# Gathering and scattering the experts' tokens with 128 rows in place of 96, the slots laid on partitions 0 to 31, 64 to 95 and 32 to 63

## The chip, the cores and the metric

The kernel runs on one core of one Trainium2 chip. The metric is the device time of one execution in microseconds (us); less is better. Three timed executions of the kernel before gave 757.03, 757.23 and 759.32 us; the median is 757.23 us.

## The reference, cut to what matters

One decoder layer for 512 prompt tokens and 32 sample tokens, T = 544 rows of D = 1024 numbers. After the attention and convolution branches and a first layer norm, each token goes through a routed mixture of 16 gated experts: a router picks one group of four experts, then two experts in it, so each token belongs to two experts and an expert has 2 * 544 / 16 = 68 tokens on average.

```python
def hier_moe(x, w_group, w_router, w1, w3, w2):
    t = x.reshape(N * S, D)
    gp = softmax(t @ w_group);  p_g, g_idx = top_k(gp, 1)
    ep = softmax((t @ w_router) of that group);  top_w, top_i = top_k(ep, 2)
    gate = one-hot sum of p_g * top_w / sum(top_w)           # (T, 16), two entries a row
    y = 0
    for e in range(16):                                      # D_EXPERT = 512
        y = y + gate[:, e:e + 1] * ((silu(t @ w1[e]) * (t @ w3[e])) @ w2[e])
x = layer_norm(ALPHA * x + hier_moe(x, ...), ln2_g, ln2_b)
```

All numbers are 32-bit floats. The weights of one expert are three matrices of 2 MB, 6 MB together (6.29 million bytes).

## The kernel before

Everything up to the first layer norm ends at about 450 us of the profiled span and is not touched, except for one small constant. The normed rows are written to a table in DRAM, `x1d`; a second table, `acc`, collects the experts' output.

**Routing.** For each token and expert the kernel has `pos`: 0 if the token does not go to the expert, otherwise its number in the expert's list, 1, 2, 3 and so on. An expert takes at most CAP = 96 tokens (a second path, not run here, treats any rest). `onehots(e)` compares `pos` with the constant `slot`, which holds 1 to 96 along the free axis, and so makes a 0/1 matrix of tokens by slots (tile `soh`). `place(e)` multiplies it with the token numbers on TensorE (L1110), and a vector operation (L1104) turns the result into row indices `gix`, one on each partition: partition p holds the token of slot p + 1. A slot without a token gets the index 1024, which is out of range; the indirect DMA has a bounds check, and such a row moves nothing. `gate_of(e, ...)` reduces the gate of each slot (L1097) and copies parts of it to other partitions with small ScalarE operations (L1099, L1101), for the use in `down`. For experts 0 and 1 `place_early` makes the indices alone, as soon as `pos` is there, and `gates_early` the gates later.

**One expert.** `gather(e)` (L1117, queue of GpSimd) reads the rows of `x1d` named by `gix` into `xg`, one row of 4 KB to a partition, 96 partitions. `x_t(e)` transposes them in 32 by 32 blocks on VectorE (L1209; on TensorE for expert 0, L1215). `up(e, ...)` multiplies with w1 and w3 on TensorE, 192 matmuls (L1229), in three rounds of 32 slots, g = 0, 1, 2; `glu` and `h_t` (L1242, L1243, L1248) make the hidden rows; `down(e, h)` multiplies with w2, 96 matmuls (L1260). Its result lies in PSUM in four partition groups of 32; six ScalarE operations (L1272, L1273 and four of L1275) scale it by the gate and bring it into `y`, 96 partitions of 4 KB. Then an indirect DMA (L1277, GpSimd) adds the rows of `y` to the rows of `acc` named by `gix`. Experts 14 and 15 make no scatter: their outputs stay in SBUF and are added by matmuls at the end (L1286, L1378, L1379).

**Order.** The program for expert e is up(e, first half), h_t(e - 1), x_t(e + 1), up(e, second half), place(e + 4) and gather(e + 4), down(e - 1), glu(e). TensorE therefore works in blocks of 192 + 96 matmuls, and the gather of an expert is issued some four experts ahead.

**Weights.** Each expert's weights come in six pieces of 1 MB: four for `up` (tile `we`, two DMAs of 512 KB each) and two for `down` (tile `wd`), all issued on SyncE's queue at L798. The pieces go round 20 buffers. From piece 21 on, a piece is issued only when the piece five before it has landed:

```python
behind = first if ring["n"] in GATED else loads[-1 - AHEAD] if ring["n"] > THR0 else None   # AHEAD = 5
```

**End.** The rows of `x1d` and `acc` are loaded into `z` (L1363, L1370, L1372; the ones from `acc` wait for the last scatter), added to the outputs of experts 14 and 15 on VectorE and ScalarE (L1426, L1430), normed and stored.

Of the kernel before, what the change touches and what calls it, by code (L numbers as in the profile page):

```python
# [18 lines left out]
F32 = mybir.dt.float32  # L19
F32R = mybir.dt.float32r  # L20
BF = mybir.dt.bfloat16
F16 = mybir.dt.float16
I32 = mybir.dt.int32
AF = mybir.ActivationFunctionType
ALU = mybir.AluOpType
AX = mybir.AxisListType.X
PSUM = bass.MemoryType.PSUM

D = 1024
# [4 lines left out]
NT = 5  # L34
# [3 lines left out]
NE = 16  # L38
# [6 lines left out]
CAP = 96  # L45
BIG = 1.0e30
FAR = 1024.0
# [31 lines left out]
YB = 2  # L79
NXG = 3  # L80
# [7 lines left out]
def layer_kernel(ctx: ExitStack, tc: tile.TileContext, i_, o_):  # L88
    nc = tc.nc
    mm = nc.tensor.matmul  # L90
# [33 lines left out]
    x1d = tc.dram_tile([T, D], F32, name="x1d")  # L124
    acc = tc.dram_tile([T, D], F32, name="acc")
    cdr = tc.dram_tile([NH, NPR], F32, name="cdr")

    const = ctx.enter_context(tc.tile_pool(name="const", bufs=1))
# [198 lines left out]
    with tc.issue_after(ln_done.ins):  # L327
# [13 lines left out]
    identb = const.tile([128, 128], BF, name="identb")  # L341
# [5 lines left out]
                            base=0, channel_multiplier=-1)  # L347
# [7 lines left out]
                            base=0, channel_multiplier=1)  # L355
    later = pa.tile([128, 128], F32, name="later")
    nc.gpsimd.affine_select(later, ones[:, :128], pattern=[[-1, 128]], compare_op=ALU.is_gt, fill=0.0,
                            base=0, channel_multiplier=1)
    before = const.tile([128, 128], BF, name="before")
    nc.gpsimd.affine_select(before, ones[:, :128], pattern=[[1, 128]], compare_op=ALU.is_gt, fill=0.0,  # L360
                            base=0, channel_multiplier=-1)
    rsel = pa.tile([NH, 4, NH, 4], F32, name="rsel")
    nc.gpsimd.affine_select(rsel, ones[:NH, :128].rearrange("p (a b c) -> p a b c", a=4, b=NH),
                            pattern=[[0, 4], [1, NH], [0, 4]], compare_op=ALU.is_equal, fill=0.0,
                            base=0, channel_multiplier=-1)
# [1 line left out]
    nc.gpsimd.iota(prow, pattern=[[0, 1]], base=0, channel_multiplier=1)  # L367
    pcol = const.tile([128, 1], F32, name="pcol")
    nc.vector.tensor_copy(pcol, prow)
    slot = const.tile([128, CAP], BF, name="slot")  # L370
    nc.gpsimd.iota(slot, pattern=[[1, CAP]], base=1, channel_multiplier=0,
                   allow_small_or_imprecise_dtypes=True)
    rn = pa.tile([128, 2], F32, name="rn")
    rni = pa.tile([128, 2], I32, name="rni")
    nc.vector.tensor_single_scalar(rni[:, 0:1], prow, 5, op=ALU.arith_shift_right)
# [4 lines left out]
                   allow_small_or_imprecise_dtypes=True)  # L380
    nc.gpsimd.iota(coln[:, 1], pattern=[[0, 8], [1, 4]], base=0, channel_multiplier=0,
                   allow_small_or_imprecise_dtypes=True)
    smask = pa.tile([128, 2, 32], BF, name="smask")
    for g in range(2):
        a = p1.tile([128, 32], F32, name="sma", tag="tra", bufs=2)
        b = p1.tile([128, 32], F32, name="smb", tag="trb", bufs=2)
        nc.vector.tensor_scalar(a, coln[:, 0].rearrange("p a b -> p (a b)"), -4.0 * g, rn[:, 0:1],
                                op0=ALU.add, op1=ALU.is_equal)
# [482 lines left out]
    xgs = []  # L871
# [21 lines left out]
    def small(name, shape, dt=F32):  # L893
        return p2.tile([128] + shape, dt, name=name)

    def bc(ap, k):
        return ap.unsqueeze(len(ap.shape)).to_broadcast(list(ap.shape) + [k])
# [189 lines left out]
    onehot = {}  # L1087

    def onehots(e):
        oh = p2.tile([128, NT, CAP], BF, name="soh", tag="soh", bufs=2)  # L1090
        nc.vector.tensor_tensor(oh, slot.unsqueeze(1).to_broadcast([128, NT, CAP]), bc(pos[:, :, e], CAP),
                                op=ALU.is_equal)
        onehot[e] = oh
        return oh

    def gate_of(e, parts):
        nc.vector.tensor_reduce(gat[:CAP, e:e + 1], parts, axis=AX, op=ALU.add)  # L1097
        if e < E0:
            nc.scalar.activation(gat2[64:, e, 0:1], gat[:64, e:e + 1], AF.Copy)  # L1099
            for q in range(4):  # L1100
                nc.scalar.activation(gat2[32 * q:32 * q + 32, e, 1:2], gat[64:96, e:e + 1], AF.Copy)  # L1101

    def to_index(e, me):
        return nc.vector.tensor_scalar(gix[:CAP, e:e + 1], me, FAR, None, op0=ALU.add)  # L1104

    def place(e):
        pmt = ps_s("pmt")
        oh = onehots(e)
        for x in range(NT):
            mm(pmt[:CAP, :5], oh[:, x], mv[:, x, e], start=x == 0, stop=x == NT - 1)  # L1110
        me = p2.tile([CAP, 1], F32, name="me", tag="me", bufs=2)
        nc.vector.tensor_reduce(me, pmt[:CAP, 0:2], axis=AX, op=ALU.add)
        to_index(e, me)
        gate_of(e, pmt[:CAP, 2:5])

    def gather(e):
        return nc.gpsimd.indirect_dma_start(out=xgs[e % NXG][:CAP], out_offset=None, in_=x1d,  # L1117
                                     in_offset=bass.IndirectOffsetOnAxis(ap=gix[:CAP, e:e + 1], axis=0),
                                     bounds_check=T - 1, oob_is_err=False)

    def place_early(e):
        oh = onehots(e)
        pm0 = ps_s("pm0")
        for x in range(NT):
            mm(pm0[:CAP, :1], oh[:, x], tokh[:, x:x + 1], start=x == 0, stop=x == NT - 1)
        return to_index(e, pm0[:CAP, :1]), gather(e)

    def gates_early(e):
        oh = onehot[e]
        pg0 = ps_s("pg0")  # L1130
        for x in range(NT):
            mm(pg0[:CAP, :3], oh[:, x], mv[:, x, e, 2:5], start=x == 0, stop=x == NT - 1)
        gate_of(e, pg0[:CAP, :3])

    gix0, first = place_early(0)
# [2 lines left out]

    gl = lgt[:, :, :NG]
    el = lgt[:, :, NG:]  # L1140
    oh1 = small("oh1", [NT, NE])
    oh2 = small("oh2", [NT, NE])
    nc.vector.scalar_tensor_tensor(oh1, rank[:, :, NG:], 0.0, asf, op0=ALU.is_equal, op1=ALU.mult)
    nc.vector.tensor_sub(oh2, asf, oh1)
    pick = p2.tile([128, NT, NE], F32, name="pick", tag="dv", bufs=2)
# [45 lines left out]
    nc.vector.tensor_reduce(flag[:1], pmT[:1, :128], axis=AX, op=ALU.max)  # L1191
    flagi = small("flagi", [1], I32)
    nc.vector.tensor_copy(flagi[:1], flag[:1])

# [59 lines left out]
    def down_round(r, py, h, raws, ks):  # L1256
        for k in ks:
            for q in range(4):
                g, c = (q % 2, 2 * (q // 2) + r) if r < 2 else (2, q)
                mm(py[32 * q:32 * q + 32, 256 * r:256 * r + 256], h[:, k, 32 * g:32 * g + 32],  # L1260
                   raws[k // 2][:, k % 2, 256 * c:256 * c + 256], start=k == 0 and r != 1, stop=k == 3,
                   skip_group_check=True)

    def down(e, h):
        y = p2.tile([CAP, D], F32, name="y", tag="y", bufs=YB)
        py = ps_mm("py").rearrange("p a b -> p (a b)")
        for j in range(2):
            raws = {j: raw_e(e, 4 + j)}
            for k in (2 * j, 2 * j + 1):
                for r in range(3):  # L1270
                    down_round(r, py, h, raws, (k,))
        nc.scalar.activation(y[:64, :512], py[:64, :512], AF.Copy, scale=gat[:64, e:e + 1])  # L1272
        nc.scalar.activation(y[:64, 512:], py[64:, :512], AF.Copy, scale=gat2[64:, e, 0:1])  # L1273
        for q in range(4):
            nc.scalar.activation(y[64:, 256 * q:256 * q + 256], py[32 * q:32 * q + 32, 512:768], AF.Copy,  # L1275
                                 scale=gat2[32 * q:32 * q + 32, e, 1:2])
        nc.gpsimd.indirect_dma_start(out=acc, out_offset=bass.IndirectOffsetOnAxis(ap=gix[:CAP, e:e + 1], axis=0),  # L1277
                                     in_=y, in_offset=None, bounds_check=T - 1, oob_is_err=False,
                                     compute_op=ALU.add)

# [8 lines left out]
    def onehots_t(e):  # L1289
        if not ohT:  # L1290
            ohT["all"] = pr_p.tile([CAP, KC, NT, 128], F32R, name="ohT", tag="pre", bufs=NPRE)
        ohp = psum.tile([CAP, NT, 128], BF, name="ohp", tag="o", bufs=1)
        for x in range(NT):
            nc.tensor.transpose(ohp[:, x], onehot[e][:, x], identb)
        ohT[e] = ohT["all"][:, e - E0]
        nc.vector.tensor_copy(ohT[e], ohp)

# [310 lines left out]
```

## Time and profile before

| what | value |
|---|---|
| median of three timed executions | 757.23 us (757.03 to 759.32) |
| the profiled execution's own time | 758.94 us |
| its span, first to last instruction | 757.2 us |
| mean granted TensorE clock | 0.987 of full speed |
| TensorE busy | 725.2 us, 96% of the span |
| DMA, mean over the span | 224 GB/s |
| chain that ended last | TensorE 68%, DMA 26%, VectorE 4% |

The page of the profile gives one execution. The busy share of TensorE is an average over stages that have different limits, and a busy TensorE is not one at its peak, since matmuls are pipelined. The time line of an engine shows runs of like instructions, with the idle time before a run in square brackets and what ended it. The DMA view of a stretch counts the packets that started in it, by queue: the loads of the weights run on q1 (issued by SyncE), the gathers and scatters on q0 (issued by GpSimd), and q8 fetches instructions. A packet's share is the time that it took; 100% stands for 16 DMA engines busy for the whole stretch, and shares add up to a little over 100% where packets of an engine overlap at their ends.

### The profile page before, as it was taken

The numbers are of one execution on the slowest core, as the hardware profiler recorded it, in microseconds if no ns is written. First come the engines' busy times: TensorE is split into PE (matmuls) and PEld (weight loads), VectorE is DVE, ScalarE is ACT, GpSimd is POOL, SyncE is SP. The second block draws the span as 40 slices with busy tenths as digits, with TensorE's granted clock in tenths as the row PEclk, the third lists the DMA queues.
The fourth block names the chain that finished last, engine by engine and source line by source line (L and its number), as shares of the span: only waits on it lengthen the run. The fifth ranks groups of instructions, "written<-read, shape, count | busy, mean of one in ns | idle before, by whom it ended". The sixth has DMA issues, their size and how long they took to land.

```text
span 757.2 us, 18645 instructions
## 1 busy us (share of the span) xinstructions
PE 725.2 (96%) x8102; PEld 563.8 (74%) x8102; DVE 354.3 (47%) x841; ACT 246.0 (32%) x502; POOL 114.7 (15%) x152
## 2 busy tenths in 40 slices
PE   7999999999999999999999998999999999898992
PEld 6899888898998999999975754656555565565551
DVE  3335667753435222333555684733454333441147
ACT  3443564533144222222423332322323322111234
POOL 5411000012441000000020521121111211100110
PEclk8999999999999999999999999999999999999997
DMA  9565302215552444434175589999999999999973
GB/s 226 188 219 173 108 29 82 70 50 194 168 168 85 144 131 147 168 112 167 57 277 182 203 327 341 339 370 337 358 371 334 363 360 338 343 375 376 386 177 121
DMA packets 65431, 169.65 MB, mean 224 GB/s; under 512 B 6144, under 2 KB 26672, under 8 KB 65344
## 3 DMA queue, kind: packets, MB, share of 16 engines
q1 hardware_dynamic: 55776, 141.08, 52.4%
q0 software_dynamic: 8992, 25.74, 12.8%
q8 instruction: 66, 1.08, 0.6%
q10 hardware_dynamic: 576, 1.57, 0.5%
q14 instruction: 21, 0.17, 0.1%
HBM read 157.40 MB, written 14.49 MB: 227 GB/s over the span
## 4 chain that ended last, share of the span: by engine, by line
PE 68%; DMA 26%; DVE 4%; issue 1%; SPq 0%; ACT 0%; DVEq 0%; ACTq 0%
DMA we<-in_w_dram 16%; PE pj L168 10%; PE pj L169 9%; PE pj L170 9%; DMA wd<-in_w_dram 8%; PE pab L1229 7%; PE py L170 2%; PE py L169 2%; PE py L168 2%; PE py L1260 2%; PE po L169 2%; PE po L170 2%; PE po L168 2%; PE py L1286 2%; PE S L566 1%; PE po L600 1%
## 5 line engine op out<-in xcount | busy, mean ns | idle before, releaser
L1229 PE MATMUL pab<-we,xgT 128*32 128x256 f32 x3072 | 172.3, 381 | 1.2 <-DMA we<-in_w_dram 1.0
L1229 PEld LDWEIGHTS pab<-we,xgT 128*32 128x32 f32 x3072 | 103.0, 111 | 65.3 <-issue 3.2
L1209 DVE STREAM_TRANSPOSE xgT<-xg 32x256 f32<-32x256 f32 x180 | 78.4, 435 | 117.1 <-PE pab L1229 106.4
L1260 PE MATMUL py<-wd,hT 128*32 128x256 f32 x1344 | 75.4, 380 | 4.5 <-DMA wd<-in_w_dram 2.9
L168 PE MATMUL pj<-xth,wgas 128*128 128x272 f32 x256 | 73.9, 289 | 0.0
L169 PE MATMUL pj<-xtl,wgas 128*128 128x272 f32 x256 | 73.9, 289 | 0.0
L170 PE MATMUL pj<-xth,wgas 128*128 128x272 f32 x256 | 73.6, 288 | 0.0
L1260 PEld LDWEIGHTS py<-wd,hT 128*32 128x32 f32 x1344 | 44.1, 110 | 30.7 <-ACT su L1242 3.8
L164 DVE TENSOR_TENSOR wgas<-wga,wgas 128x1024 fp32r<-128x1024 f32 x16 | 19.6, 1226 | 87.3 <-ACT wgas L163 87.3
L168 PEld LDWEIGHTS pj<-xth,wgas 128*128 128x128 f32 x256 | 48.3, 189 | 0.8 <-issue 0.8
L169 PEld LDWEIGHTS pj<-xtl,wgas 128*128 128x128 f32 x256 | 48.2, 188 | 0.0
L170 PEld LDWEIGHTS pj<-xth,wgas 128*128 128x128 f32 x256 | 48.2, 188 | 0.0
L1242 ACT ACTIVATE su<-pab 128x384 f32<-128x384 f32 x16 | 7.8, 490 | 104.8 <-PE pab L1229 104.8
L1277 POOL DMA_INDIRECT acc<-y,gix x14 | 20.1, 1439 | 129.0 <-ACT y L1275 129.0
L168 PE MATMUL pj<-xth,wqks 128*128 128x272 f32 x128 | 38.6, 302 | 0.0
L169 PE MATMUL pj<-xtl,wqks 128*128 128x272 f32 x128 | 36.9, 289 | 0.0
L170 PE MATMUL pj<-xth,wqks 128*128 128x272 f32 x128 | 36.9, 289 | 0.0
L163 ACT ACTIVATE wgas<-wga 128x1024 fp32r<-128x1024 f32 x16 | 16.9, 1055 | 47.4 <-DMA wga<-in_w_in_dram 46.5
L1117 POOL DMA_INDIRECT xg<-x1d,gix x16 | 15.7, 980 | 101.9 <-DVE gix L1104 76.5
L1272 ACT ACTIVATE y<-py,gat 64x512 f32<-64x512 f32 x14 | 9.5, 682 | 64.5 <-PE py L1260 36.1
L840 ACT ACTIVATE sg<-pj 128x544 f32<-128x544 f32 x16 | 9.9, 617 | 54.4 <-PE pj L170 53.8
L169 PE MATMUL po<-wos,mxh 128*128 128x512 f32 x64 | 26.0, 406 | 0.9 <-DVE wos L164 0.9
(426 smaller groups left out, 1560.8 us busy)
## 6 DMA issues: line engine op xcount, KB each, us to landing
we<-in_w_dram SPq DMA_DIRECT2D x128, 512.0 KB, 14.0
wd<-in_w_dram SPq DMA_DIRECT2D x32, 1024.0 KB, 16.0
wga<-in_w_in_dram SPq DMA_DIRECT2D x8, 1024.0 KB, 6.7
wqk<-in_w_in_dram SPq DMA_DIRECT2D x4, 1024.0 KB
wo<-in_w_o_dram SPq DMA_DIRECT2D x4, 1024.0 KB, 5.0
xa<-in_x_prompt_dram SPq DMA_DIRECT2D x4, 512.0 KB, 11.8
ckb<-cdr POOLq DMA_DIRECT2D x8, 256.0 KB, 3.7
wcg<-in_w_in_dram SPq DMA_DIRECT2D x2, 1024.0 KB
```

The lines of the kernel that those rows point to most:

```text
L163: nc.scalar.activation(h, src, AF.Copy)
L164: (eng or nc.vector).tensor_sub(l, src, h.bitcast(F32))
L168: mm(out, al, bh, start=first, stop=False)
L169: mm(out, ah, bl, start=False, stop=False)
L170: return mm(out, ah, bh, start=False, stop=last)
L840: nc.scalar.activation(h2(e), pm, AF.Sigmoid)
L1117: return nc.gpsimd.indirect_dma_start(out=xgs[e % NXG][:CAP], out_offset=None, in_=x1d, in_offset=bass.IndirectOffsetOnAxis(ap=gix[:CAP, e ...
L1209: nc.vector.transpose(x[32 * j:32 * j + 32, :, 32 * g:32 * g + 32].rearrange("p (j r) s -> p j r s", r=2), rows[32 * g:32 * g + 32, :, :, ...
L1229: mm(out[32 * c:32 * c + 32], x[:, k, 32 * g:32 * g + 32], rhs[:, :, :, c], start=k == 0 and g != 1, stop=k == 7, skip_group_check=True)
L1260: mm(py[32 * q:32 * q + 32, 256 * r:256 * r + 256], h[:, k, 32 * g:32 * g + 32], raws[k // 2][:, k % 2, 256 * c:256 * c + 256], start=k == ...
L1277: nc.gpsimd.indirect_dma_start(out=acc, out_offset=bass.IndirectOffsetOnAxis(ap=gix[:CAP, e:e + 1], axis=0), in_=y, in_offset=None, bounds ...
L1286: pe_last.append(mm(py[:CAP], h[:, k], raws[k // 2][:, k % 2, n * 512:(n + 1) * 512], start=k == 0, stop=k == 3))
```

## The change

The constant `slot` has 128 entries: partition block 0 to 31 gets slots 1 to 32, block 32 to 63 gets slots 65 to 96, block 64 to 95 gets slots 33 to 64, and block 96 to 127 gets -1, which no token has. So the first 32 tokens of an expert lie on partitions 0 to 31, the next 32 on 64 to 95, and what is over on 32 to 63; partitions 96 to 127 always carry the index out of range. The index tile, the gather and the scatter go over 128 partitions in place of 96. The one-hot matrix is 128 columns wide. Since matmul round g works on partitions 32g to 32g + 31, as before, `down_round` and the scaling operations exchange the second and the third block: the scaling of `y` becomes eight ScalarE operations (two of 32 by 512 where there was one of 64 by 512), and `gate_of` has one small copy more. The two `y` buffers are made once, and their last 32 partitions are cleared on GpSimd (two memsets) before the loop. The one-hots `oh1`, `oh2` of the gate computation share a buffer with other tiles.

```diff
--- before.py
+++ after.py
@@ -367,9 +367,12 @@
     nc.gpsimd.iota(prow, pattern=[[0, 1]], base=0, channel_multiplier=1)
     pcol = const.tile([128, 1], F32, name="pcol")
     nc.vector.tensor_copy(pcol, prow)
-    slot = const.tile([128, CAP], BF, name="slot")
-    nc.gpsimd.iota(slot, pattern=[[1, CAP]], base=1, channel_multiplier=0,
-                   allow_small_or_imprecise_dtypes=True)
+
+    slot = const.tile([128, 128], BF, name="slot")
+    for b, first_slot in enumerate((1, 65, 33)):
+        nc.gpsimd.iota(slot[:, 32 * b:32 * b + 32], pattern=[[1, 32]], base=first_slot, channel_multiplier=0,
+                       allow_small_or_imprecise_dtypes=True)
+    nc.gpsimd.memset(slot[:, 96:], -1.0)
     rn = pa.tile([128, 2], F32, name="rn")
     rni = pa.tile([128, 2], I32, name="rni")
     nc.vector.tensor_single_scalar(rni[:, 0:1], prow, 5, op=ALU.arith_shift_right)
@@ -1087,8 +1090,8 @@
     onehot = {}
 
     def onehots(e):
-        oh = p2.tile([128, NT, CAP], BF, name="soh", tag="soh", bufs=2)
-        nc.vector.tensor_tensor(oh, slot.unsqueeze(1).to_broadcast([128, NT, CAP]), bc(pos[:, :, e], CAP),
+        oh = p2.tile([128, NT, 128], BF, name="soh", tag="soh", bufs=2)
+        nc.vector.tensor_tensor(oh, slot.unsqueeze(1).to_broadcast([128, NT, 128]), bc(pos[:, :, e], 128),
                                 op=ALU.is_equal)
         onehot[e] = oh
         return oh
@@ -1096,40 +1099,41 @@
     def gate_of(e, parts):
         nc.vector.tensor_reduce(gat[:CAP, e:e + 1], parts, axis=AX, op=ALU.add)
         if e < E0:
-            nc.scalar.activation(gat2[64:, e, 0:1], gat[:64, e:e + 1], AF.Copy)
+            for b in (0, 64):
+                nc.scalar.activation(gat2[b + 32:b + 64, e, 0:1], gat[b:b + 32, e:e + 1], AF.Copy)
             for q in range(4):
-                nc.scalar.activation(gat2[32 * q:32 * q + 32, e, 1:2], gat[64:96, e:e + 1], AF.Copy)
+                nc.scalar.activation(gat2[32 * q:32 * q + 32, e, 1:2], gat[32:64, e:e + 1], AF.Copy)
 
     def to_index(e, me):
-        return nc.vector.tensor_scalar(gix[:CAP, e:e + 1], me, FAR, None, op0=ALU.add)
+        return nc.vector.tensor_scalar(gix[:, e:e + 1], me, FAR, None, op0=ALU.add)
 
     def place(e):
         pmt = ps_s("pmt")
         oh = onehots(e)
         for x in range(NT):
-            mm(pmt[:CAP, :5], oh[:, x], mv[:, x, e], start=x == 0, stop=x == NT - 1)
-        me = p2.tile([CAP, 1], F32, name="me", tag="me", bufs=2)
-        nc.vector.tensor_reduce(me, pmt[:CAP, 0:2], axis=AX, op=ALU.add)
+            mm(pmt[:, :5], oh[:, x], mv[:, x, e], start=x == 0, stop=x == NT - 1)
+        me = p2.tile([128, 1], F32, name="me", tag="me", bufs=2)
+        nc.vector.tensor_reduce(me, pmt[:, 0:2], axis=AX, op=ALU.add)
         to_index(e, me)
         gate_of(e, pmt[:CAP, 2:5])
 
     def gather(e):
-        return nc.gpsimd.indirect_dma_start(out=xgs[e % NXG][:CAP], out_offset=None, in_=x1d,
-                                     in_offset=bass.IndirectOffsetOnAxis(ap=gix[:CAP, e:e + 1], axis=0),
+        return nc.gpsimd.indirect_dma_start(out=xgs[e % NXG], out_offset=None, in_=x1d,
+                                     in_offset=bass.IndirectOffsetOnAxis(ap=gix[:, e:e + 1], axis=0),
                                      bounds_check=T - 1, oob_is_err=False)
 
...
@@ -1256,25 +1261,30 @@
     def down_round(r, py, h, raws, ks):
         for k in ks:
             for q in range(4):
-                g, c = (q % 2, 2 * (q // 2) + r) if r < 2 else (2, q)
+                g, c = (q // 2 * 2, 2 * (q % 2) + r) if r < 2 else (1, q)
                 mm(py[32 * q:32 * q + 32, 256 * r:256 * r + 256], h[:, k, 32 * g:32 * g + 32],
                    raws[k // 2][:, k % 2, 256 * c:256 * c + 256], start=k == 0 and r != 1, stop=k == 3,
                    skip_group_check=True)
 
+    ys = [p2.tile([128, D], F32, name="y", tag="y", bufs=YB) for _ in range(YB)]
+    for y in ys:
+        nc.gpsimd.memset(y[96:], 0.0)
+
     def down(e, h):
-        y = p2.tile([CAP, D], F32, name="y", tag="y", bufs=YB)
+        y = ys[e % YB]
         py = ps_mm("py").rearrange("p a b -> p (a b)")
         for j in range(2):
             raws = {j: raw_e(e, 4 + j)}
             for k in (2 * j, 2 * j + 1):
                 for r in range(3):
                     down_round(r, py, h, raws, (k,))
-        nc.scalar.activation(y[:64, :512], py[:64, :512], AF.Copy, scale=gat[:64, e:e + 1])
-        nc.scalar.activation(y[:64, 512:], py[64:, :512], AF.Copy, scale=gat2[64:, e, 0:1])
+        for b in (0, 64):
+            nc.scalar.activation(y[b:b + 32, :512], py[b:b + 32, :512], AF.Copy, scale=gat[b:b + 32, e:e + 1])
+            nc.scalar.activation(y[b:b + 32, 512:], py[b + 32:b + 64, :512], AF.Copy, scale=gat2[b + 32:b + 64, e, 0:1])
         for q in range(4):
-            nc.scalar.activation(y[64:, 256 * q:256 * q + 256], py[32 * q:32 * q + 32, 512:768], AF.Copy,
+            nc.scalar.activation(y[32:64, 256 * q:256 * q + 256], py[32 * q:32 * q + 32, 512:768], AF.Copy,
                                  scale=gat2[32 * q:32 * q + 32, e, 1:2])
-        nc.gpsimd.indirect_dma_start(out=acc, out_offset=bass.IndirectOffsetOnAxis(ap=gix[:CAP, e:e + 1], axis=0),
+        nc.gpsimd.indirect_dma_start(out=acc, out_offset=bass.IndirectOffsetOnAxis(ap=gix[:, e:e + 1], axis=0),
                                      in_=y, in_offset=None, bounds_check=T - 1, oob_is_err=False,
                                      compute_op=ALU.add)
 
...
```

Left out of the diff: `place_early`, `gates_early` and `onehots_t` take 128 or 96 columns of the wider one-hot in the same way, and `oh1`, `oh2` become the two halves of one tile.

## Rows read from the trace of the kernel before

**Rows 1.** The page, part 2: busy share of the DMA engines in 40 slices.
```profile
DMA  9565302215552444434175589999999999999973
```

**Rows 2.** Stages: busy us of each engine (instructions), clock, DMA share, GB/s.
```profile
620.00:640.00 20.00, 20.00 (x373) 12.04 (x369) 6.50 (x17) 3.71 (x7) 3.85 (x3) 1.00 1.01 352
640.00:660.00 20.00, 19.27 (x349) 11.34 (x339) 6.63 (x18) 3.85 (x8) 2.42 (x2) 1.00 0.98 330
660.00:680.00 20.00, 17.10 (x316) 12.21 (x320) 9.05 (x21) 4.07 (x8) 1.42 (x1) 1.00 1.01 379
680.00:700.00 20.00, 17.93 (x324) 11.81 (x320) 4.09 (x9) 3.72 (x7) 1.40 (x1) 1.00 1.03 379
700.00:720.00 20.00, 19.83 (x253) 11.04 (x248) 2.81 (x4) 4.59 (x8) 2.05 (x2) 1.00 1.02 383
```

**Rows 3.** Time line of TensorE at two blocks: start, us, what.
```profile
568.35 10.54 PE L1229 MATMUL pab<-we,xgT 128*32 128x256 f32 x192
578.82 0.39 PE L1110 MATMUL pmt<-mv,soh 128*96 128x5 bf16 x5
579.14 5.39 PE L1260 MATMUL py<-wd,hT 128*32 128x256 f32 x96
584.34 10.54 PE L1229 MATMUL pab<-we,xgT 128*32 128x256 f32 x192
```

**Rows 4.** Time line of TensorE from 640 us; idle time before it in brackets.
```profile
648.32 2.77 PE L1229 MATMUL pab<-we,xgT 128*32 128x256 f32 x48
...
661.25 5.39 PE L1260 MATMUL py<-wd,hT 128*32 128x256 f32 x96 [1.45 <-DMA wd<-in_w_dram]
...
678.65 5.39 PE L1260 MATMUL py<-wd,hT 128*32 128x256 f32 x96 [1.65 <-DVE su L1243]
...
697.05 5.39 PE L1260 MATMUL py<-wd,hT 128*32 128x256 f32 x96 [1.45 <-DMA wd<-in_w_dram]
702.23 5.39 PE L1229 MATMUL pab<-we,xgT 128*32 128x256 f32 x96
```

**Rows 5.** What the queue of SyncE waited for, 500 to 700 us: us, times, longest.
```profile
SPq L798 <- DMA we<-in_w_dram: 96.3, 50, 4.2
...
SPq L798 <- PE pab L1229: 0.8, 3, 0.4
```

**Rows 6.** The chain that ended last, 495 to 735 us: start, us, what.
```profile
525.68 16.22 DMA wd<-in_w_dram
...
697.00 12.63 DMA wd<-in_w_dram
```

**Rows 7.** DMA queues, 612 to 616 us: packets, MB, share of 16 engines.
```profile
q1 hardware_dynamic: 433, 1.62, 100.9%
```

**Rows 8.** DMA queues, 616 to 619 us: a gather is under way.
```profile
q1 hardware_dynamic: 151, 0.56, 66.1%
q0 software_dynamic: 111, 0.34, 40.1%
```

**Rows 9.** DMA queues, 592.4 to 596.4 us: a scatter is under way.
```profile
q0 software_dynamic: 112, 0.26, 32.9%
```

**Rows 10.** The same scatter, a step of half a us (592.9 to 593.4).
```profile
q0 software_dynamic: 11, 0.05, 45.0%
```

**Rows 11.** DMA queues, 33 to 37 us: gathers of 128 cache rows beside loads.
```profile
q0 software_dynamic: 238, 0.78, 51.9%
```

**Rows 12.** ScalarE by form, 440 to 757 us: busy us, mean ns, idle before.
```profile
L1272 ACT ACTIVATE y<-py,gat 64x512 f32<-64x512 f32 x14 | 9.5, 682 | 64.5 <-PE py L1260 36.1 <-issue 28.4
```

**Rows 13.** All engines around the first gather.
```profile
448.50 1.22 DVE L1091 TENSOR_TENSOR soh<-slot,pos 128x480 bf16<-128x480 bf16 x2
...
456.97 1.32 PE L1215 MATMUL xgT<-ident,xg 96*128 96x96 f32 x7 [3.96 <-DMA xg<-x1d,gix]
```

**Rows 14.** Instructions that issue the gathers: ns min/median/max, first and last start.
```profile
L1117 POOL DMA_INDIRECT xg<-x1d,gix x16: 952/981/1047, 450.7 to 643.9; - x16
```

**Rows 15.** Time line of GpSimd: clearing a tile of 128 partitions.
```profile
381.47 0.96 POOL L874 MEMSET xg<- 128x1024 f32 x1 [141.63 <-DVE mix L825]
```

More of the change, by code (lines that the diff above doesn't have):

```diff
@@ L1124, in place_early @@
         for x in range(NT):
-            mm(pm0[:CAP, :1], oh[:, x], tokh[:, x:x + 1], start=x == 0, stop=x == NT - 1)
-        return to_index(e, pm0[:CAP, :1]), gather(e)
+            mm(pm0[:, :1], oh[:, x], tokh[:, x:x + 1], start=x == 0, stop=x == NT - 1)
+        return to_index(e, pm0[:, :1]), gather(e)
     def gates_early(e):
@@ L1131, in gates_early @@
         for x in range(NT):
-            mm(pg0[:CAP, :3], oh[:, x], mv[:, x, e, 2:5], start=x == 0, stop=x == NT - 1)
+            mm(pg0[:CAP, :3], oh[:, x, :CAP], mv[:, x, e, 2:5], start=x == 0, stop=x == NT - 1)
         gate_of(e, pg0[:CAP, :3])
@@ L1140, in layer_kernel @@
     el = lgt[:, :, NG:]
-    oh1 = small("oh1", [NT, NE])
-    oh2 = small("oh2", [NT, NE])
+    picks = p2.tile([128, 2, NT, NE], F32, name="picks", tag="su", bufs=1)
+    oh1, oh2 = picks[:, 0], picks[:, 1]
     nc.vector.scalar_tensor_tensor(oh1, rank[:, :, NG:], 0.0, asf, op0=ALU.is_equal, op1=ALU.mult)
@@ L1293, in onehots_t @@
         for x in range(NT):
-            nc.tensor.transpose(ohp[:, x], onehot[e][:, x], identb)
+            nc.tensor.transpose(ohp[:, x], onehot[e][:, x, :CAP], identb)
         ohT[e] = ohT["all"][:, e - E0]
```

## The prediction, made before the changed kernel was run

> **What bounds the kernel now.** I read the page first: the DMA engines are 90% busy or more from slice 23 to slice 38, while the experts run [rows 1]. Then the stages: up to 640 us TensorE is busy all the time, 20.00 of 20 us; from 640 to 720 us it is busy 19.27 + 17.10 + 17.93 + 19.83 = 74.13 of 80 us [rows 2]. So there are two limits, one after the other. The time line shows each. Undisturbed, a block of TensorE (192 matmuls of `up`, 5 of `place`, 96 of `down`) takes 584.34 - 568.35 = 15.99 us [rows 3]. From 640 us on, TensorE stops ahead of `down` and waits for a piece of the weights [rows 4]; the stop of 1.65 us is put down to a VectorE operation, but the chain at that time consists of weight loads. That chain steps from load to load, from 525.68 us to the landing of the one issued at 697.00 us [rows 6]: each load waits for the landing of the one five before, 50 waits and 96.3 us on `we` alone, and hardly ever for a buffer, 0.8 us [rows 5]. The weights start with a lead on TensorE, lose it expert by expert, and from about 650 us on TensorE waits.
>
> What can be gained at this place: three blocks without `place` run from 648.32 to 702.23, 53.91 us [rows 4]. Undisturbed they take 3 * (15.99 - 0.32) = 47.0 us; 0.32 us is the time from the first matmul of `place` at 578.82 to the first of `down` at 579.14 [rows 3]. That is **6.9 us** of waiting, and TensorE can't be served better than that.
>
> **What the transfers cost.** Where weights alone move, 1.62 MB are 396 packets of 4 KB, and 100.9% of 16 engines for 4 us is 64.6 us: 163 ns a packet, and 405 GB/s [rows 7]. While a gather runs, 0.56 MB of weights (137 packets) take 66.1% of 48 us, 31.7 us, and 0.34 MB of rows (83) take 19.2 us: 232 ns for either [rows 8]. So gathered rows and loads obstruct each other: 220 * (232 - 163) ns = 15.2 us of engine time, 0.95 us on each of 16 engines for 83 rows, about 0.8 us for the average 68. A scattered row takes 327 ns: 11 rows, 45.0% of 8 us [rows 10]. The whole scatter moves 0.26 MB, 63 rows, in 21.06 us; its other 49 packets (33 rows out of range, 16 completions) take what is left, 0.46 us, 9 ns each [rows 9]. Eleven rows start in a step of half a us [rows 10], which is one on each of eleven engines: 63 = 10 * 6 + 3. So 96 rows are dealt out in six neighbours to an engine, and with 63 rows five engines get none. Per expert, an engine with full shares spends 6 * 163 + 6 * 327 ns = 2.9 us on rows, the idle five nothing, and the weights, dealt evenly, wait for the slowest.
>
> **The change, part by part.**
>
> *The rows over 16 engines.* With 128 partitions an engine has eight. The trace before shows no DMA of 128 rows with some out of range, so the deal has to be bounded. If an engine's eight partitions are four neighbours in one block and four in another, the new slot order gives every engine 4 rows of the first 64 tokens, and the rest go to engines that hold parts of block 32 to 63. Four rows for six save 2 * (163 + 327) ns = 1.0 us per expert; the one engine with slots 65 to 68 keeps 4 or 8, on average about six, and saves nothing. If the deal is eight neighbours, eight engines carry 8 rows and lose 1.0 us per expert.
>
> *The obstruction.* Whether 128 rows obstruct the loads is bounded below by nothing saved and above by 0.8 us per gather. The nearest row is near the upper end: gathers of 128 cache rows beside loads take 51.9% of 64 us for 0.78 MB (190 packets), 175 ns [rows 11], against 232. I take all of it.
>
> So over some 13 experts the slowest engine saves 13 * 0.8 = 10 us (the one with 8 rows) to 13 * 1.8 = 23 us (the others). Only 6.9 us are needed: the loads keep their lead to the end, and TensorE sets the time. The saving is therefore cut to 6.9 us, whichever engine is the slowest.
>
> The Trainium skill, "DMA: Bandwidth & Descriptors", section "The descriptor swizzle", gives an engine four partitions and the four 32 further on, and so 0 to 63 to engines 0 to 7; by it the deal is 4 and 4 and the sum stays 6.9 us. No run here shows it for an indirect DMA. The same page, section "Bandwidth", speaks against the change: HBM gives a core about 358 GB/s, whatever the engines do; by it the sum would be 0. The stages move 330 to 383 GB/s [rows 2], close to that, but the 405 GB/s of weights alone [rows 7] don't agree with it.
>
> *Rows out of range.* 32 more per DMA at 9 ns, over 16 engines: 0.02 us per DMA. Nothing.
>
> *ScalarE.* Two operations of 0.68 us become four over half the partitions; a price by the free length gives 2 * 0.68 = 1.4 us more per expert, by partitions nothing. I take 1.4 us. ScalarE sits idle 64.5 us ahead of these 14 groups, 4.6 us each [rows 12], and the next thing behind them on its queue is the `glu` of the next block, so they are covered; without the cover they would cost 14 * 1.4 = 19 us. What comes later by 1.4 us is the scatter; no matmul waits for it before the end, where the loads of `acc` wait for the last one. The additional gate copy is a fraction of the same idle time.
>
> *The first gather.* Two one-hots took 1.22 us for 480 columns [rows 13]; 640 make it 1.63 us, 0.4 us later on the path to the first gather. TensorE waited 3.96 us for that gather [rows 13]; four rows for six on the engines save two rows of each of two gathers, 4 * 163 to 4 * 232 ns, so 0.3 us (if only the first one's two count) to 0.9 us. I take the two effects as equal, 0; the ends are 0.9 us less (the one-hots covered) and 0.4 us more (nothing saved). Later one-hots hide behind 16 us blocks.
>
> *GpSimd.* Issuing a gather of 96 rows took 0.98 us [rows 14]; by the number of rows that becomes 1.31 us at most, on an engine that mostly waits for indices: nothing. The two clears of `y` are at most 0.96 us each [rows 15], on the same queue; behind them are the gathers of experts 2 and 3, needed 16 us later. If they came ahead of the first gather, and late, they would cost up to 1.9 us. The longer `slot` is made in the first 20 us, ahead of a wait.
>
> **The sum.** The profiled execution took 758.94 us for a span of 757.2 us; it lies 1.7 us above the median. 758.94 - 6.9 = 752.0 us on that execution, and 757.23 - 6.9 = **750.3 us** on the median. What TensorE does after its last wait, and the norm at the end, only move forward.
>
> **The rivals.**
>
> *Part of the waiting stays* (15%): the engine with 8 rows falls behind in the fullest experts, or half of the obstruction stays, and 2 to 4.5 us of 6.9 are left: 752.3 to 754.8 us. For it: that engine saves only the obstruction. Against it: 10 us saved against 6.9 needed.
>
> *Bytes bind, not rows per engine* (9%): the loads arrive as before and the waits of [rows 4] stay; 757.2 us, and up to 756 or 758.5 by the first gather and the clears. By the HBM figure cited above it comes out so; the 405 GB/s speak against it.
>
> *Eight neighbours to an engine* (10%), the slower side: engines that hold blocks 0 to 31 and 64 to 95 carry 8 rows of every expert. They lose 13 * 1.0 = 13 us; with the obstruction gone 13 - 10 = 3 us. Since TensorE already waits at the end, all of it is lost: 760 to 770 us. It decides as soon as more is lost per expert than the 0.8 us of obstruction saved. For it: 96 rows are dealt in neighbours. Against it: gathers of 128 rows ran unobstructed.
>
> **How the numbers follow.** My forecast has 66%: 750.3 us, its own range 749.2 us (the first gather's 0.9 us, and the 0.17 us idle in the last stage [rows 2]) to 752.3 us. The range, with 0.2 us for the spread of the runs below their median, is 749.0 to 757.2 us: it holds nearly all of the forecast, the first rival and half of the second. 0.3% is 2.3 us, about what a measurement of this kernel can tell from no change. Faster than 754.96 us are the forecast and nearly all of the first rival, 0.80; within 0.3% the second, with a remainder of the first, 0.10; slower 0.10.
>
> **What would show it right or wrong.** In the profile after: TensorE busy 20 of 20 us in the stages from 640 to 700 us; in a gather's stretch, packets near 163 to 180 ns, not 232; in a scatter's, up to sixteen rows starting in a step, not eleven; the queue of SyncE waiting for buffers (TensorE) near the end, not only for loads. Wrong would be the same waits ahead of `down`; a scatter with eight or nine rows in a step shows the deal in neighbours. If loads are early and the time is still not 7 us less, a wait of TensorE on ScalarE or on the gathers has taken their place.

## The result, and the profile after

In a comparison on one chip the changed kernel took 750.93 us (median of 4, 750.16 to 752.15) and the kernel before 757.62 us (median of 4): ratio 0.991, 95% interval 0.989 to 0.993, 6.7 us less. The profiled execution took 752.15 us, its span is 750.4 us.

The stages after, from the same view as [rows 2]:

```profile
620.00:640.00 20.00, 20.00 (x377) 11.93 (x373) 6.50 (x17) 7.61 (x14) 3.81 (x3) 1.00 1.03 389
640.00:660.00 20.00, 20.00 (x377) 11.93 (x373) 6.52 (x18) 5.09 (x10) 3.03 (x3) 1.00 1.02 385
660.00:680.00 20.00, 20.00 (x376) 12.03 (x372) 10.66 (x24) 5.54 (x10) 1.56 (x1) 1.00 1.03 383
680.00:700.00 20.00, 20.00 (x376) 12.09 (x372) 3.17 (x7) 8.66 (x15) 1.55 (x1) 1.00 0.97 371
700.00:720.00 20.00, 20.00 (x169) 9.82 (x159) 4.06 (x6) 4.34 (x8) 5.45 (x6) 1.00 0.75 177
```

TensorE, the first engine, is busy 20.00 of 20 us in all of them; no stage shows the 17.10 or 17.93 us of [rows 2]. The last stage moves 177 GB/s, since the last weights land at about 700 us. The time line of TensorE has no bracket any more, at the place of [rows 4] and at that of [rows 3]:

```profile
564.50 0.28 PE L1114 MATMUL pmt<-mv,soh 128*128 128x5 bf16 x5
...
580.39 0.28 PE L1114 MATMUL pmt<-mv,soh 128*128 128x5 bf16 x5
...
649.37 10.54 PE L1234 MATMUL pab<-we,xgT 128*32 128x256 f32 x192
659.73 5.36 PE L1265 MATMUL py<-wd,hT 128*32 128x256 f32 x96
...
695.99 5.36 PE L1234 MATMUL pab<-we,xgT 128*32 128x256 f32 x96
```

Three blocks without `place` take 695.99 - 649.37 = 46.62 us, where [rows 4] have 53.91. A block with `place` takes 580.39 - 564.50 = 15.89 us, where [rows 3] have 15.99: `place` itself got shorter, 0.28 for 0.39 us, which the prediction does not have.

The DMA queues while a gather is under way (first fence, 617 to 620 us, as [rows 8]) and in half a us of a scatter (second, 596.0 to 596.5 us, as [rows 10]):

```profile
q1 hardware_dynamic: 234, 0.88, 72.8%
q0 software_dynamic: 139, 0.34, 28.9%
```

```profile
q0 software_dynamic: 16, 0.07, 65.4%
```

In the gather, 0.88 MB are 215 packets in 72.8% of 48 us: 162 ns a load, where it was 232. The 0.34 MB of rows are 83 packets; less 0.5 us for 56 small packets they took 13.4 us, 161 ns each. The obstruction is gone. In the scatter sixteen rows start in half a us, not eleven, at 65.4% of 8 us / 16 = 327 ns each as before: a row is no faster, but all sixteen engines carry rows at once.

What SyncE waited for, 500 to 700 us, as [rows 5]:

```profile
SPq L801 <- DMA we<-in_w_dram: 83.8, 50, 4.2
...
SPq L801 <- PE pmt L1114: 3.0, 3, 2.0
SPq L801 <- PE py L1265: 2.9, 4, 1.1
...
SPq L801 <- PE pab L1234: 1.2, 3, 0.5
```

The loads still wait mostly for each other, because that is how they are chained, but now 7.1 us of the waits are for TensorE to free a buffer: the loads run against the kernel's own pace. From the issue of the first gather to the issue of the last four pieces of `we` it is 678.28 - 453.12 = 225.2 us, where it was 699.55 - 450.65 = 248.9 us: on this stretch the loads gained 23.7 us. The chain that ended last is 88% TensorE and 5% DMA (before: 68% and 26%).

One thing got worse. The time line of GpSimd ahead of the first gather:

```profile
441.24 0.95 POOL L1271 MEMSET y<- 32x1024 f32 x1 [5.42 <-DMA acc<-x]
442.28 2.34 POOL L998 TENSOR_TENSOR x<-x,xg 128x1024 f32<-128x1024 f32 x1
447.42 0.95 POOL L1271 MEMSET y<- 32x1024 f32 x1 [2.80 <-DMA x1d<-x]
453.12 1.09 POOL L1121 DMA_INDIRECT xg<-x1d,gix  x1 [4.75 <-DMA we<-in_w_dram]
```

The first clear of `y` waits 5.42 us for a DMA that still reads the buffer's last owner, and the addition of L998 stands behind it; it began at 438.40 us before, now at 442.28. The first gather is issued at 453.12 us instead of 450.7 [rows 14]. VectorE is caught up in it as well:

```profile
442.69 1.96 DVE L982 SCALAR_TENSOR_TENSOR asb<-rank,goh 128x16 bf16<-128x16 f32 x1
```

This operation takes 0.17 us where it runs alone; here it lasts to 442.69 + 1.96 = 444.65, the end of GpSimd's addition at 444.62. The Trainium skill ("SBUF — State Buffer", section "SBUF: two separate sides") has a pair of ports that VectorE and GpSimd share, locked by one of them for a whole instruction; this row agrees with it.

The first gather waits for indices that stand at the end of the VectorE operations behind this one. Their one-hots began at 448.50 us before [rows 13], and now:

```profile
450.69 1.55 DVE L1094 TENSOR_TENSOR soh<-slot,pos 128x640 bf16<-128x640 bf16 x2
```

Of these 2.19 us, 0.47 were there already at the third addition (432.05 us, before 431.58), so 1.7 us came in between. By these times it is through VectorE that the clears reach the first gather.

### The profile page after: what moved, and what is told of

It reads as the page before. It is cut to its first block, busy times and chain, and to the rows that moved or that the text cites. A ratio compares the mean times of both kernels' runs of the same rounds, so it can differ in the third digit from the quotient of the medians.

```text
span 750.4 us, 18691 instructions
## 1 busy us (share of the span) xinstructions
PE 722.8 (96%) x8102; PEld 557.3 (74%) x8102; DVE 358.5 (48%) x841; ACT 267.8 (36%) x544; POOL 119.8 (16%) x157
## 4 chain that ended last, share of the span: by engine, by line
PE 88%; DMA 5%; DVE 5%; ACT 1%; issue 1%; SPq 0%; DVEq 0%; ACTq 0%
PE pab L1234 23%; PE py L1265 10%; PE pj L168 10%; PE pj L169 9%; PE pj L170 9%; DMA wqk<-in_w_in_dram 3%; PE py L170 2%; PE py L169 2%; PE py L168 2%; PE po L169 2%; PE py L1296 2%; PE po L170 2%; PE po L168 2%; PE S L569 2%; PE po L603 1%; PE ptp L592 1%
## 5 line engine op out<-in xcount | busy, mean ns | idle before, releaser
L1234 PEld LDWEIGHTS pab<-we,xgT 128*32 128x32 f32 x3072 | 99.9, 111 | 66.9 <-issue 2.1
L1265 PEld LDWEIGHTS py<-wd,hT 128*32 128x32 f32 x1344 | 42.5, 110 | 27.2
L1287 POOL DMA_INDIRECT acc<-y,gix x14 | 22.2, 1587 | 136.7 <-ACT y L1285 122.7
L1282 ACT ACTIVATE y<-py,gat 32x512 f32<-32x512 f32 x28 | 19.0, 677 | 57.5 <-PE py L1265 31.0
L163 ACT ACTIVATE wgas<-wga 128x1024 fp32r<-128x1024 f32 x16 | 16.9, 1055 | 46.7 <-DMA wga<-in_w_in_dram 45.8
```

The lines of the kernel that those rows point to most:

```text
L163: nc.scalar.activation(h, src, AF.Copy)
L1234: mm(out[32 * c:32 * c + 32], x[:, k, 32 * g:32 * g + 32], rhs[:, :, :, c], start=k == 0 and g != 1, stop=k == 7, skip_group_check=True)
L1282: nc.scalar.activation(y[b:b + 32, :512], py[b:b + 32, :512], AF.Copy, scale=gat[b:b + 32, e:e + 1])
```

## The experiments

In the three sessions of the experiments the kernel before took 766.2 to 767.7 us, 8.5 to 10 us more than in the first comparison. The kernel after took 7.9 us more in the session in which it ran again, and 7.7 of them lie ahead of the experts (the addition of L998 that begins at 432.05 us in its first profile begins at 439.76 in its second). So results are compared by their ratio to the kernel before, which ran beside them. Between sessions even this ratio moved: one kernel that ran in two of them had 0.9917 and 0.9864 (experiment 4). A difference of half a per cent between ratios of two sessions therefore shows nothing by itself.

**1. The order alone.** The new slot order and the clears, but 96 rows, in the gather as shown and in the scatter in the same way:

```diff
-        return nc.gpsimd.indirect_dma_start(out=xgs[e % NXG], out_offset=None, in_=x1d,
-                                     in_offset=bass.IndirectOffsetOnAxis(ap=gix[:, e:e + 1], axis=0),
+        return nc.gpsimd.indirect_dma_start(out=xgs[e % NXG][:CAP], out_offset=None, in_=x1d,
+                                     in_offset=bass.IndirectOffsetOnAxis(ap=gix[:CAP, e:e + 1], axis=0),
```

> The new slot order, but gathers and scatters of 96 rows. Theory A (the rows must be dealt to the engines in two groups of four, and the 128 rows also stop the obstruction of the loads; both come from the 128 rows): rows are dealt six neighbours to an engine as before, gathered rows and loads take about 232 ns beside each other, TensorE keeps some 6 us of waits ahead of down after 640 us; 757 us, give or take 1.5 (about 2 lost at the start by the clears, about 1 won by the 128-column matmuls of place, as in the kernel after). Rival O (the order of the slots alone spreads the load): the waits go, 751 us.

Measured: 767.09 us, ratio 1.0014 (1.0003 to 1.0025). Most of the waits are still there: the three blocks without `place` take 711.14 - 659.17 = 51.97 us, 5.4 more than in the kernel after. The brackets on TensorE's time line:

```profile
674.29 2.80 PE L1265 MATMUL py<-wd,hT 128*32 128x256 f32 x48 [1.33 <-DMA wd<-in_w_dram]
691.41 2.80 PE L1265 MATMUL py<-wd,hT 128*32 128x256 f32 x48 [1.34 <-DMA wd<-in_w_dram]
708.50 2.80 PE L1265 MATMUL py<-wd,hT 128*32 128x256 f32 x48 [1.30 <-DMA wd<-in_w_dram]
```

Its DMA queues in a gather, 628 to 630 us:

```profile
q1 hardware_dynamic: 112, 0.41, 70.6%
q0 software_dynamic: 68, 0.20, 34.5%
```

0.41 MB are 100 loads in 70.6% of 32 us, 226 ns each: obstructed. Theory A stands, rival O falls.

**2. The width alone.** 128 rows, the slots in plain order; matmul rounds, scaling and gate copies go with it as in the kernel before:

```diff
-    for b, first_slot in enumerate((1, 65, 33)):
+    for b, first_slot in enumerate((1, 33, 65)):
```

> Gathers and scatters of 128 rows, but slots 1 to 96 in plain order on partitions 0 to 95. Theory A (two groups of four rows to an engine, partition p with p + 32): eight engines then carry 8 rows of the first 64 tokens, lose 2 * (163 + 327) ns = 1.0 us per expert and win 0.8 us by the loads that are not obstructed, so the waits of TensorE near the end stay or grow: 756 to 761 us. Rival W (the obstruction is all that mattered, the order of the slots is of no use): no waits, 751 us. In both the packets in the stretch of a gather should be near 160 ns.

Measured: 767.72 us, ratio 1.0020 (1.0009 to 1.0031), so 1.5 us slower than the kernel before. The three blocks without `place` take 711.84 - 657.99 = 53.85 us, as in the kernel before: all of the waits are there, and rival W falls. Its queues in a gather (594 to 597 us) and in half a us of a scatter (605 to 605.5 us):

```profile
q1 hardware_dynamic: 262, 0.99, 80.7%
q0 software_dynamic: 63, 0.22, 18.1%
```

```profile
q1 hardware_dynamic: 39, 0.13, 65.8%
q0 software_dynamic: 8, 0.03, 32.7%
```

The loads are not obstructed (242 in 80.7% of 48 us, 160 ns), but only eight rows start in half a us: eight engines. So 8, 11 and 16 rows start in half a us with 128 rows in plain order, with 96 rows, and with 128 rows in the new order. This fits the deal that the prediction used, four partitions and the four that are 32 further on. Eight neighbours are ruled out, since by them the new order would start eight rows as well; which four partitions of a block go together, these counts don't tell. Neither part alone makes the kernel faster; both together do.

**3. What the transfers alone would do.** Since TensorE caps the gain, the four layouts ran again with half of the matmuls of `up` and `down` left out, and then, in another session, two more in which only the gathers or only the scatters are wide (the lines shown are of `down`; those of `up` change in the same way):

```diff
-            for k in (2 * j, 2 * j + 1):
+            for k in (2 * j,):
```

> The kernel before, leaving out half of the matmuls of up and down (every second k); all weights are still loaded. TensorE then needs some 8 us for an expert, and the transfers alone set the pace. They set it already in the kernel before (loads chained from load to load from 525 us on), so the time is only some 5 to 10 us less than 757: about 749 us, with the last weights landing near 715 to 720 us.

> The kernel after, leaving out the same half of the matmuls. Theory A (13 experts by 0.8 us of obstruction, and for all engines but one 1.0 us of rows): the loads end 10 to 23 us earlier than in the halved kernel before; 726 to 739 us. Rival (bytes bind): no difference beyond 2 us.

> 128 rows with the slots in plain order, half of the matmuls left out. Theory A (eight rows on each of eight engines): within 4 us of the halved kernel before, rather slower (13 * 0.2 = 2.6 us). Rival W (the obstruction alone counts): about 10 us less than the halved kernel before, and as fast as the halved kernel after.

> 96 rows in the new order, half of the matmuls left out. Theory A: as the halved kernel before, within 2 us, since six neighbours still go to an engine. Rival O (the order alone spreads the rows): 10 us less or more.

> Half of the matmuls left out; gathers of 128 rows, scatters of 96, new order. Of the 16.9 us between the halved kernels before and after, the working of the prediction gives a gather 0.8 us of obstruction and 2 rows of 163 ns per expert, a scatter 2 rows of 327 ns: 1.13 to 0.65. So the gathers should bring 63% of it: 10.7 us less than the halved kernel before, with a ratio to the kernel before of 1.001. Rival (the scatter is what holds up the loads): under 6 us less.

> Half of the matmuls left out; gathers of 96 rows, scatters of 128, new order. By the same working the scatters bring 37%: 6.2 us less than the halved kernel before, with a ratio to the kernel before of 1.007. Rival (the scatter is what holds up the loads): over 10 us less.

| half of the matmuls left out | us | ratio to the kernel before | GB/s, 500 to 700 us | first gather to last `we`, us |
|---|---|---|---|---|
| before: 96 rows | 776.82 | 1.0151 (1.0081 to 1.0220) | 362 | 243.9 |
| 96 rows, new order | 776.93 | 1.0152 (1.0089 to 1.0216) | 360 | 243.0 |
| 128 rows, plain order | 779.53 | 1.0186 (1.0116 to 1.0256) | 354 | 244.2 |
| 128 rows in scatters, new order | 773.32 | 1.0072 (1.0045 to 1.0098) | 371 | 237.9 |
| 128 rows in gathers, new order | 762.45 | 0.9930 (0.9908 to 0.9952) | 382 | 228.8 |
| after: 128 rows, new order | 759.88 | 0.9935 (0.9903 to 0.9967) | 388 | 227.4 |

The GB/s are from these rows, one for the halved kernel before and one for the halved kernel after:

```profile
500.00:700.00 200.00, 128.23 (x1783) 64.06 (x1779) 83.45 (x203) 51.86 (x121) 27.35 (x22) 0.86 1.01 362
```

```profile
500.00:700.00 200.00, 126.66 (x1857) 64.47 (x1850) 84.98 (x203) 74.38 (x160) 31.96 (x24) 0.93 1.03 388
```

The last column is from the time lines of GpSimd and SyncE, again for the halved kernel before and the halved kernel after:

```profile
457.73 1.05 POOL L1117 DMA_INDIRECT xg<-x1d,gix  x1 [9.89 <-DVE m L1148]
701.64 4.92 SPq L798 DMA_DIRECT2D we<-in_w_dram  x4
```

```profile
459.15 1.10 POOL L1121 DMA_INDIRECT xg<-x1d,gix  x1 [4.46 <-DVE over L1187]
686.54 3.35 SPq L801 DMA_DIRECT2D we<-in_w_dram  x4
```

TensorE is busy 128 and 127 of 200 us, so the transfers set the pace, and at nearly the same DMA share (1.01 and 1.03) they move 362 and 388 GB/s. TensorE's mean granted clock is lower than 1.00 in these rows, 0.86 and 0.93, but the stretch of the last column ends with loads, not with matmuls. The whole change is worth 776.82 - 759.88 = 16.9 us of transfers, and 243.9 - 227.4 = 16.5 us by the last column, within the 10 to 23 us forecast. The order alone changes the time by 0.1 us. The plain order is 2.7 us slower, as the 2.6 forecast would have it, but two runs of each, some 3 us apart, can't tell that from nothing. Its GB/s are lower, while by the last column its loads come as fast as before (244.2 for 243.9 us). So what eight rows on an engine cost stays open. The gathers bring more than the 63% expected: by GB/s (382 - 362) / 26 = 77%, by the last column 15.1 of 16.5 us, by the ratios all of it. The scatters alone bring 6.1 us by the ratio (6.2 expected), 6.0 by the last column and 35% by GB/s, but next to wide gathers hardly anything that these few runs can tell. The rival that the scatters hold up the loads falls.

One expectation failed: the halved kernels should have been faster than the whole ones by 5 to 10 us, and without the wide gathers they are slower, with them no faster (the halved kernel after 759.88 us, the whole one 758.87). SyncE's time line of the halved kernel with 96 rows in the new order, and below that of the whole kernel with the same layout (experiment 1):

```profile
704.84 3.39 SPq L801 DMA_DIRECT2D we<-in_w_dram  x4
708.69 4.14 SPq L1373 DMA_DIRECT2D z<-x1d  x3
719.59 0.78 SPq L1380 DMA_DIRECT2D z<-acc  x2
720.42 2.22 SPq L801 DMA_DIRECT2D wd<-in_w_dram  x2
```

```profile
708.53 3.35 SPq L801 DMA_DIRECT2D we<-in_w_dram  x4
713.62 2.91 SPq L801 DMA_DIRECT2D wd<-in_w_dram  x2
716.63 3.69 SPq L1373 DMA_DIRECT2D z<-x1d  x3
```

The last `we` is only 3.7 us earlier with half of the matmuls, which confirms that the loads set their own pace; but in the halved kernel the loads of `z`, some of which wait for the last scatter, stand ahead of the last two pieces of `wd`, and those are issued 6.8 us later. That is the same in all halved kernels and leaves their comparison intact.

**4. The clears behind the second gather.**

```diff
-    for y in ys:
-        nc.gpsimd.memset(y[96:], 0.0)
+    with tc.issue_after(second.ins):
+        for y in ys:
+            nc.gpsimd.memset(y[96:], 0.0)
```

> The kernel after, with the two clears of y told to stand behind the second early gather on GpSimd's queue. Theory C (the clears, which wait 5.4 us for a DMA that read the buffer's last owner, push the last x1 addition on GpSimd and through it the first gather): the first gather is issued about 2.5 us earlier, near 450.7 us, and the time falls by 1.7 to 2.2 us, to about 749. Rival (TensorE waits for the weights or for something else as soon as it starts earlier, or the one-hots of 640 columns are what came later): the time stays within 0.5 us of the kernel after, 751.

> The kernel after once more, beside the kernel with the late clears on one chip, so that the two can be told apart. Ratio to the kernel before 0.991, as in the first comparison.

> The kernel with the late clears, beside the kernel after on one chip. Its first look showed the first gather issued 2.9 us earlier than where the clears stand in front, and all else alike. Theory C: 1.7 to 2.9 us less than the kernel after, ratio to the kernel before 0.987 to 0.989. Rival (what is won at the start is lost again further on): no difference over 0.5 us.

GpSimd's time line in the first run:

```profile
445.47 2.37 POOL L998 TENSOR_TENSOR x<-x,xg 128x1024 f32<-128x1024 f32 x1 [3.04 <-DVE asb L982]
458.00 1.09 POOL L1121 DMA_INDIRECT xg<-x1d,gix  x1 [10.16 <-DMA we<-in_w_dram]
459.40 1.00 POOL L1121 DMA_INDIRECT xg<-x1d,gix  x1 [0.30 <-DVE pg L1162]
460.44 1.97 POOL L1272 MEMSET y<- 32x1024 f32 x2
```

From the third addition of L998 (438.64 us here, 432.05 in the kernel after, 431.58 before) to the first gather are 19.36 us, against 21.07 in the kernel after and 19.1 before: the mechanism is shown, and 1.7 us come back. In the first session the late clears gave 758.90 us, ratio 0.9917 (0.9899 to 0.9934), no better than the 0.991 of the kernel after in the first comparison, where about 0.989 had been expected; the kernel after was not beside it. Side by side, in the second: after 758.87 us (757.64 to 759.71), ratio 0.9880 (0.9864 to 0.9896), somewhat more than in the first comparison, so that the change is worth 7 to 9 us; late clears 757.41 us (756.89 to 758.21), ratio 0.9864 (0.9846 to 0.9883). The difference of 1.5 us is a little less than the 1.7 to 2.9 expected, and the first gather is 1.90 us earlier (459.30, 461.20); but the intervals overlap, so the gain at the start is shown, and that in the whole time only likely. By its median beside the kernel after it is the fastest version.

**5. A narrow `place`.** The matmuls of `place` over 96 columns of the one-hot, the last 32 indices set once:

```diff
-            mm(pmt[:, :5], oh[:, x], mv[:, x, e], start=x == 0, stop=x == NT - 1)
+            mm(pmt[:CAP, :5], oh[:, x, :CAP], mv[:, x, e], start=x == 0, stop=x == NT - 1)
```

> The kernel after, with the matmuls of place over 96 columns of the one-hot, and the last 32 indices set once to 1024. Theory P (96 columns of stationary data in place of 128 are what made place and the switch to down take 0.32 us in place of 0.21): every block takes 15.99 in place of 15.89 us, and with 12 to 14 places the time rises by 1.2 to 1.5 us over the kernel after, to about 752.3. Rival (the shorter place has another reason, such as the weights of down lying ready): no change, 751.

Measured: 760.58 us, ratio 0.9933 (0.9908 to 0.9957), against 0.9880 (0.9864 to 0.9896) for the kernel after in the other session. TensorE's time line:

```profile
556.30 0.39 PE L1115 MATMUL pmt<-mv,soh 128*96 128x5 bf16 x5
...
572.30 0.39 PE L1115 MATMUL pmt<-mv,soh 128*96 128x5 bf16 x5
```

Since the ratios are from two sessions, they don't decide it. The block does: it is at 16.00 us again, 0.39 us of it `place`, so theory P stands. The cause lies in the loads of the stationary columns, by form, 96 columns (this kernel) and 128 (after); after the bar busy us and mean ns:

```profile
L1115 PEld LDWEIGHTS <-soh 128*96 128x96 bf16 x70 | 4.2, 123 | 5.8 <-issue 4.9 <-DVE soh L1095 0.4 <-DVE gix L1118 0.4
```

```profile
L1114 PEld LDWEIGHTS <-soh 128*128 128x128 bf16 x70 | 2.7, 96 | 5.8 <-issue 4.9 <-DVE gix L1108 0.4 <-DVE soh L1094 0.4
```

More columns load faster, 96 ns for 123. The Trainium skill ("TensorE: Matmul & The Clock Gate", section "Weight-path perf modes — Fast Weight Load (FWL) and DoubleRow") has the compiler turn on a fast weight load at 128 columns that are not 32-bit floats; the rows agree.

## Why the prediction was right

- *What bounds it, 6.9 us to be gained at the end.* Right. 53.91 us became 46.62, 7.3 us. 47.0 had been forecast; the rest is that `up` goes over to `down` a little sooner than to `place` (659.73 - 649.37 = 10.36 us, where [rows 3] have 10.47 up to `place`).
- *The rows over 16 engines.* Right, and shown by the 8, 11 and 16 rows that start in half a us. The rival of eight neighbours falls by the sixteen rows. The width alone does load eight engines with eight rows; that rival had 13 * 0.2 us lost there, net of the obstruction, and the halved kernel shows 2.7 us in the time, within the noise, and 0.3 us in the loads, so this price stays open.
- *The obstruction, all of it taken.* Right: 226 to 232 ns with 96 rows, 160 to 162 ns with 128, in either order. Why 96 rows obstruct the loads stays open.
- *10 to 23 us saved, cut to 6.9 by TensorE.* Right: 16.9 us with half of the matmuls, and 23.7 us in the loads of the whole kernels. The share of the gathers was put too small (63%, measured 77% and more), that of the scatters too large.
- *Bytes bind.* Refuted: the halved kernels before and after move the same weights and rows, and the one takes 16.9 us less.
- *ScalarE, covered.* Right: the group of 32 by 512 takes 677 ns, as much as that of 64 by 512, so the additional operations do cost the forecast 1.4 us per expert, and no matmul waits for them: from 470 to 735 us TensorE waits once, 1.1 us for a VectorE operation at the end, as it did before.
- *The first gather and the clears, 0.* Mis-sized: 1.2 us were lost where 0 had been put in. The one-hots cost 0.33 us more (0.4 forecast) and the gathered rows came 0.7 us sooner (453.12 to 458.67, before 450.7 to 456.97); but the clears, which the prediction priced at up to 1.9 us only if they came first and late, did come first and late. From the third addition of L998 to the first transposition it is 26.62 us instead of 25.39.
- *`place`, not costed at all.* 0.1 us less each of the 14 times that it runs.
- *TensorE's clock after the wait for the first gather, not costed either.* The first 96 matmuls of `up` took 467.37 - 460.16 = 7.21 us, before 464.85 - 458.39 = 6.46. TensorE had stood idle for 3.49 us ahead of the transpositions before it (3.96 us before); its granted clock was 0.50 (1.2 GHz) from 460 to 464 us, where before it was 0.81 from 460 to 462 us and 1.00 (2.4 GHz) from there on. Why it rose later this time, no run shows.

So from the first transposition to the end of the span it is 291.7 us instead of 300.2: 8.5 us less. They are 7.29 us of the three blocks, 1.47 of `place` and 0.56 behind the three blocks, less 0.82 at the first matmuls. Ahead of it 1.7 us are lost: 1.2 between the third addition and the first transposition (1.7 by the clears and 0.3 by the one-hots, less 0.7 by the sooner rows), and 0.5 before the third addition, for which these runs give no reason. 8.5 - 1.7 = 6.8 us, the difference of the spans. The mechanism was right, but that the sum of 6.9 was met so closely is luck: what it did not hold, some 2.4 us of gains (0.4 more in the three blocks, the 1.47 and the 0.56) and 2.5 us of losses (0.8 and 1.7), nearly cancelled.

## What to carry to other kernels

When loads share the DMA engines with row gathers and scatters, count the engines that carry rows, by the rows that start in a short stretch, and look whether the loads' packets get longer beside them: a gather made wider with rows that move nothing can be faster for everything else. Put clears of a reused buffer behind the work that is on the path, since they inherit the wait of the buffer's last owner. And take what the bounding engine wins as the cap of the gain: here 16.9 us of transfers bought 6.7 us.

## What the runs showed of the hardware that was not expected

- In a gather of 96 rows beside loads, the packets of both took 225 to 232 ns; in one of 128 rows, 45 of which moved nothing in the kernel after, 160 to 162 ns.
- A load of 128 stationary columns of bf16 took 96 ns, one of 96 columns 123 ns.
- A VectorE operation of 0.17 us took 1.96 us beside a GpSimd addition, to the end of that addition.
